# High and low parts of split weight blocks in one tile and one transfer

## The chip, the cores and the metric

The kernel runs on one NeuronCore of a Trainium2 chip. The metric is the device time of one execution in microseconds (us). Three runs of the kernel before gave 1211.52, 1212.36 and 1213.43 us; their median, 1212.36 us, is the time before. Engines are named as the profile names them: PE (TensorE) multiplies, PEld is its weight load, DVE (VectorE), ACT (ScalarE) and POOL (GpSimd) work elementwise, SP (SyncE) issues transfers. ACT and POOL issue transfers too; "SPq" and "ACTq" are those issues.

## The reference

One layer of a hybrid decoder step over 1024 prompt rows and 8 x 8 sample rows (1088 columns in all), model width 1024, float32:

```
h    = rmsnorm(x) * (1 + scale) + shift            # scale, shift, gate from silu(c) @ w_ada + b_ada
proj = h @ w_in                                    # 1024 -> 8224: u_pool, z_pool, z_ssm, xBC, dt, g
P    = (pool_mix(u_pool) * silu(z_pool)) @ w_pool_out          # 512 -> 1024
S    = gated_rmsnorm(SSD(conv(xBC)) + D*x, z_ssm) @ w_ssm_out  # 2048 -> 1024
x    = x + gate * ((sigmoid(g_pool) * P + sigmoid(g_ssm) * S) @ w_o)
out  = rmsnorm(x), and the new pooling, convolution and SSD states
```

SSD is a chunked state-space scan: 4 groups of heads, 8 chunks of 128 rows each.

## The kernel before, in words

**High and low parts.** Every float32 operand of a large product is split into a high part (a copy rounded to the fast float32r format, made by ACT) and a low part (operand minus high part, made by POOL or DVE). A product is then three products: high x high, low x high, high x low. A weight block is 128 x 512 numbers on 128 partitions, 2 KB a partition and 256 KB in all, for each part.

**Stages, in order of time.** (1) The first stage, up to about 90 us, has its order on all engines written out by hand. (2) Pairs of `w_in` columns go through a Strassen scheme (`strassen`, `product`, matmuls on line 411). Each block is split by `split` (line 142; ACT line 145, POOL line 148) into a `whi` and a `wlo` tile; the pool `wp` holds four of each, in turn. (3) Beside these pairs, `splits` (line 262) prepares `w_pool_out` and `w_ssm_out`: 40 blocks, each loaded (`begin`, line 275), scaled by the norm's gain and rounded (`halve`, lines 283 and 284), reduced to its low part on POOL (line 286), and stored to memory. `halve` stores the high part (line 285), `end` stores the low part (line 290), three steps later; a step is one product of 24 matmuls. All three issue on ACT's queue, and the raw tile `pw` has two buffers, the high tile `ph` has one. (4) From about 745 us the SSD chunks run, woven on PE with the products of the 40 prepared blocks (`gemm_`, matmuls on line 221). `ready` (line 304) loads each block's two parts back with two loads on SP's queue (lines 308 and 309), two units ahead of its use. (5) In the same stage `wo_splits` (line 1766) forms the Strassen sums of `w_o` on DVE (lines 1793 to 1804), 20 pieces of 128 x 512. `part` rounds a piece into a tile `ph` (three buffers, ACT line 1771), stores it on ACT's queue (line 1772), and POOL subtracts in place (line 1773). `out` stores the low part on SP's queue one step later (line 1778). (6) The tail multiplies by `w_o` and writes the outputs; there the buffers of `whi` and `wlo` are reused for the gate (`ga`), the sample rows (`sh`) and output rows (`w4`).

**What a chunk needs.** `chunk` (line 1492) loads `dec` (line 1225) three chunks ahead into one of three buffers; then ACT (lines 1504 and 1233), POOL (line 1229) and DVE (lines 1529 and 1531) turn it into the operands of `inner` (PE lines 1245 and 1248).

**Who sets the order.** In stages 1 and 4 to 5 the order on PE and SP is the order of the program text (`in_line`). Elsewhere, and on ACT, DVE and POOL in stages 4 to 6, a planner in the compiler orders instructions by a simulated timeline, with buffers of a tag handed out in turn when their last user is done. Each engine then runs its list strictly in order, its transfer issues included: an issue that waits for a buffer holds up what stands behind it on that engine.

Of the kernel before, what the change touches and what calls it, by code (L numbers as in the profile page):

```python
# [8 lines left out]
F32 = mybir.dt.float32  # L9
F32R = mybir.dt.float32r  # L10
AF = mybir.ActivationFunctionType
ALU = mybir.AluOpType
# [8 lines left out]
P = 128  # L21
# [25 lines left out]
def tile_pool_ssd_step(  # L47
# [5 lines left out]
    nc = tc.nc  # L53
    uid = [0]

    def nm(s):
        uid[0] += 1
        return f"{s}_{uid[0]}"

    cp = ctx.enter_context(tc.tile_pool(name="cp", bufs=1))  # L60
    wp = ctx.enter_context(tc.tile_pool(name="wp", bufs=3))
# [28 lines left out]
    def R(shape=(P, T), dt=F32):  # L90
        return hs.tile(list(shape), dt, tag="R", name=nm("R"), bufs=3)

    def Y4(pool, dt=F32R):
        return pool.tile([P, 4, T], dt, tag="Y", name=nm("Y"), bufs=2)
# [14 lines left out]
    load = nc.sync.dma_start  # L109
    store_ = nc.scalar.dma_start  # L110
    mm = nc.tensor.matmul
    act = nc.scalar.activation
# [26 lines left out]
    vT = const([P, 44], "vT")  # L139
    pscl = vT[:, 40:44]  # L140

    def split(raw, kept=None, ncols=P, eng=None):
        hi = wp.tile([P, 4, P], F32R, tag="whi", name=nm("whi"), bufs=4)
        lo = wp.tile([P, 4, P], F32R, tag="wlo", name=nm("wlo"), bufs=4)
        ins = act(hi[:, :, :ncols], raw[:, :, :ncols], AF.Copy)  # L145
        if kept is not None:
            kept.append(ins.ins)
        (eng or nc.gpsimd).tensor_tensor(lo[:, :, :ncols], raw[:, :, :ncols], hi[:, :, :ncols].bitcast(F32), ALU.subtract)  # L148
        return hi, lo
# [87 lines left out]
    def dram(name, shape, dt=F32):  # L237
        return dr.tile(list(shape), dt, tag=name, name=name)
# [23 lines left out]
    def splits():  # L262
        jobs = [(w_pool_out[m], None, wp_d[m]) for m in range(8)]
        jobs += [(w_ssm_out[g, m], 24 + 4 * g, ws_d[g][m])
                 for g in range(NG) for m in range(8)]
        raws, made = {}, [0]

        def paced():

            return highs[min(made[0] + 3, len(highs) - 1)]  # L270

        def begin(n):
            raws[n] = gas[0].tile([P, 4, P], F32, tag="pw", name=nm("pw"), bufs=2)
            with tc.issue_after(paced()):
                store_(raws[n], jobs[n][0])

        def halve(n):
            raw, gain = raws[n], jobs[n][1]
            hi = gas[0].tile([P, 4, P], F32R, tag="ph", name=nm("ph"), bufs=1)
            with tc.issue_after(paced()):  # L280
                if gain is not None:
                    for k in range(4):
                        act(raw[:, k], raw[:, k], AF.Copy, scale=vT[:, gain + k:gain + k + 1])
                act(hi, raw, AF.Copy)  # L284
                store_(jobs[n][2][:, 0], hi.bitcast(F32))
            nc.gpsimd.tensor_tensor(raw.bitcast(F32R), raw, hi.bitcast(F32), ALU.subtract)  # L286

        def end(n):
            with tc.issue_after(paced()):
                store_(jobs[n][2][:, 1], raws.pop(n))  # L290
        at = {}
        for n in range(len(jobs)):
            for f, step in ((end, 5), (begin, 0), (halve, 2)):
                at.setdefault(n * 17 // 5 + step, []).append((f, n))
        for t in range(max(at) + 1):
            made[0] += 1
            for f, n in sorted(at.get(t, ()), key=lambda x: x[1]):
                f(n)
            yield

    def wtiles():
        return [wp.tile([P, 4, P], F32R, tag=t, name=nm(t), bufs=4) for t in ("whi", "wlo")]

    def ready(d):
        def ws():
            with tc.high_priority(PRI):
                hi, lo = wtiles()
                load(hi.bitcast(F32), d[:, 0])
                load(lo.bitcast(F32), d[:, 1])
            return [(hi, lo)]  # L310
        return ws


# [197 lines left out]
    gas = []  # L511
# [113 lines left out]
    def first():  # L625
# [166 lines left out]
        raws, w, banks = {}, {}, {}  # L792
# [4 lines left out]
            load(raws[t, j], tiles_of(c)[:, 4 * j:4 * j + 4])  # L797

        def pieces(x, at):
            w[at] = [wp.tile([P, 4, P], F32R, tag=t, name=nm(t), bufs=4) for t in ("whi", "wlo")]  # L800
            return act(w[at][0], x, AF.Copy)

        def hi(t, j):
            pieces(raws[t, j], (t, j))
# [228 lines left out]
        def loads():  # L1033
            while waiting and said.issuperset(waiting[0][0]):
# [3 lines left out]
                     hi=hi, lo=lo, pr=pr, sgt=lambda: None, sg=sg, dwd=dwd, dU=dU, dL=dL, dR=dR, dUo=dUo,  # L1038
# [11 lines left out]
        for word in ORDER1:  # L1050
            fs = word.split(".")
            name, args = fs[0], [int(a) if a.isdigit() else a for a in fs[1:]]
            if name not in calls:
                i = len(name.rstrip("0123456789"))
                args.insert(0, int(name[i:]))
                name = name[:i]
# [396 lines left out]


    hst = [None] * NG

    CKL = ("sz", "v")

    def ckt(shape, tag, bufs=2):
        return (cl if tag in CKL else ca if tag in ("dec", "xb", "cE", "bc") else ck).tile(list(shape), F32, tag=tag, name=nm(tag), bufs=bufs)  # L1460
# [240 lines left out]
    cl = open_("cl", 2)  # L1701
    right = tc.tile_pool(name="ck", bufs=2, side="right", reuse_waits="tile")
    ck = right.__enter__()
    for shape, tag, bufs in (((P, 512), "ph", 3), ((P, P), "bt", 2), ((P, 8, 64), "xd", 2), ((P, 8, 64), "xw", 1),
                             ((P, 4, NS), "szs", 1), ((P, 512), "t2", 1), ((P, 512), "hst", 2)):
        ckt(shape, tag, bufs)

# [55 lines left out]
    wo_d = [dram(f"wo{k}", [P, 2, 4, 512]) for k in range(5)]  # L1763
    oB11, oT3, oT2, oT1, oT4 = range(5)

    def wo_splits():
        outs = []

        def part(o, k, t):
            hi = ck.tile([P, 512], F32R, tag="ph", name=nm("ph"), bufs=3)  # L1770
            act(hi, t, AF.Copy)
            store_(wo_d[o][:, 0, k], hi.bitcast(F32))
            nc.gpsimd.tensor_tensor(t.bitcast(F32R), t, hi.bitcast(F32), ALU.subtract)
            outs.append((wo_d[o][:, 1, k], t))

        def out():
            while outs:
                load(*outs.pop(0))
        left_, right_ = slice(0, 512), slice(512, 1024)

        def row(o):
            t = R()
            load(t[:, :D], w_o[0, o:o + P, :])
            return t
        up, dn = row(0), None
        yield
        for k in range(4):
            out()
            if k:
                part(oT3, k - 1, dn[:, right_])  # L1790
            old, dn = dn, row(512 + k * P)
            yield
            V.tensor_tensor(dn[:, right_], dn[:, right_], up[:, right_], ALU.subtract)
            V.tensor_tensor(up[:, right_], up[:, right_], up[:, left_], ALU.subtract)
            out()
            if k:
                part(oT4, k - 1, old[:, left_])
            yield
            t2 = ckt([P, 512], "t2", 1)
            V.tensor_tensor(t2, dn[:, right_], up[:, left_], ALU.add)  # L1800
            out()
            part(oT1, k, up[:, right_])
            yield
            V.tensor_tensor(dn[:, left_], t2, dn[:, left_], ALU.subtract)
            out()
            part(oB11, k, up[:, left_])
            yield
            out()
            part(oT2, k, t2)
            if k < 3:  # L1810
                up = row(k * P + P)
            yield
        out()
        part(oT3, 3, dn[:, right_])
        yield
        out()
        part(oT4, 3, dn[:, left_])
        yield
        out()
# [59 lines left out]
    def M(shape=(P, T), dt=F32):  # L1879
        return mp.tile(list(shape), dt, tag="m", name=nm("m"), bufs=2)  # L1880
# [10 lines left out]
    for o, n in GB:  # L1891
        s = slice(o, o + n)
# [18 lines left out]
    def b_load(o, y):  # L1911
        for t, c in ((0, lo_), (1, up_)):
            load(y[:, :, c].bitcast(F32), wo_d[o][:, t])
        return y
# [70 lines left out]
        return (pf, run)  # L1985
    run_units([tail_unit(m) for m in range(8)])

    def w2k(tag, dt=F32):
        return wp.tile([P, 512], dt, tag=tag, name=nm("half"), bufs=4)
    yt2 = b_load(oT2, Y4(hs))  # L1990

    lows = Y4(hs)
# [2 lines left out]
        nc.gpsimd.tensor_tensor(s2l[:, k], acc[k][:, lo_], s2h[:, k].bitcast(F32), ALU.subtract)  # L1995
    for k in range(4):
        nc.gpsimd.tensor_tensor(s1l[:, k], acc[k][:, up_], s1h[:, k].bitcast(F32), ALU.subtract)
    ga = [w2k("whi"), w2k("whi")]
    for half in range(2):
        load(ga[half], gate_d[0:1, half * 512:half * 512 + 512].squeeze(0).partition_broadcast(P))  # L2000

    sh = []
    for j in range(2):
        t = wp.tile([P, 4, P], F32R, tag="whi", name=nm("sh"), bufs=4)
        for k in range(4):
            a = acc[4 * j + k][:, SEQ:]
            act(t[:, k, 0:NS], a, AF.Copy)
            V.tensor_tensor(t[:, k, NS:P], a, t[:, k, 0:NS].bitcast(F32), ALU.subtract)
        sh.append(t)
# [6 lines left out]

    top = [R() for _ in range(3)] + [hs.tile([P, T], F32, tag="sq", name="top3", bufs=1)]
    C1 = [(t[:, lo_], t[:, up_]) for t in top]
    w4 = [w2k("wlo") for _ in range(4)]
    C2 = [(w4[0], w4[1]), (w4[2], w4[3])] + [(t[:, lo_], t[:, up_]) for t in (M(), M())]  # L2020
    bank = [0]

# [90 lines left out]
    for half in range(2):  # L2113
        c = slice(half * 512, half * 512 + 512)
# [168 lines left out]
```

## Time and profile before

| | |
|---|---|
| three runs, median | 1212.36 us |
| the profiled execution, device time | 1210.91 us |
| its span, first to last instruction | 1209.2 us |
| mean granted PE clock | 0.999 |
| instructions | 25239 |
| bytes read and written in memory | 173.31 MB, 87.73 MB |

The profile is of one execution. Its device time is 1.7 us more than its span. A row such as `L145 ACT ACTIVATE whi<-rawA` names a line of the kernel, the engine, the operation, and the tile written from the tile read. Busy time is the time in which an engine had an instruction of the program running; matmuls overlap each other, and their ends are modelled.

### The profile page before, as it was taken

What the parts mean: (1) busy time and instruction counts of PE and PEld (TensorE: products, weight loads), DVE (VectorE), ACT (ScalarE), POOL (GpSimd) and SP (SyncE); (2) the same over time, 40 slices, a digit from 0 to 9 for tenths busy, and PEclk for the clock granted to TensorE, in tenths of its full rate; (3) what the DMA queues carried; (4) which work ended last, traced back from release to release, by engine and by line L of the source; (5) the groups of instructions that cost most, each with busy time, mean ns of one, the idle gap of its engine ahead of it and who ended that gap; (6) DMA issues with size and microseconds to landing.
All of it is one profiled execution on the core that took longest, in us unless ns stands there. A gap on an engine that the chain in (4) does not pass through costs nothing.

```text
span 1209.2 us, 25239 instructions
## 1 busy us (share of the span) xinstructions
PE 1194.4 (99%) x9242; PEld 1118.5 (93%) x9242; DVE 924.8 (76%) x1535; ACT 649.1 (54%) x1479; POOL 763.4 (63%) x655
## 2 busy tenths in 40 slices
PE   9999999999999999999999999999999999999997
PEld 8879999999999999999989999988888888999885
DVE  6993788877989578877576555687878889679976
ACT  6864356565666557454434334566676657312435
POOL 1137878875988787764777776255767758423653
PEclk9999999999999999999999999999999999999999
DMA  9836445574556455454667767988879888585794
GB/s 352 306 132 219 136 144 184 164 228 146 171 174 198 160 164 172 135 169 131 208 227 238 245 223 247 320 309 262 270 250 294 277 284 285 173 326 166 235 212 154
DMA packets 167924, 262.72 MB, mean 217 GB/s; under 512 B 32880, under 2 KB 80760, under 8 KB 167800
## 3 DMA queue, kind: packets, MB, share of 16 engines
q1 hardware_dynamic: 90408, 166.01, 41.9%
q10 hardware_dynamic: 73232, 87.16, 21.2%
q0 software_dynamic: 4160, 7.94, 3.2%
q8 instruction: 73, 1.20, 0.4%
q14 instruction: 51, 0.42, 0.1%
HBM read 173.31 MB, written 87.73 MB: 216 GB/s over the span
## 4 chain that ended last, share of the span: by engine, by line
PE 87%; DVE 5%; DMA 3%; ACT 2%; issue 1%; POOL 0%; ACTq 0%; DVEq 0%; SPq 0%; POOLq 0%
PE mm L411 24%; PE ps L411 23%; PE mm L221 17%; PE pc L411 5%; PE ps L1245 3%; PE pc L1536 2%; PE ps L1248 2%; PE ps L2036 2%; PE ps L2034 2%; PE ps L2035 2%; PE ps L1511 1%; DMA dec<-acs_d 1%; DMA Y<-in_x_prompt 1%; PE ps L957 1%; DVE tf L643 1%
## 5 line engine op out<-in xcount | busy, mean ns | idle before, releaser
L148 POOL TENSOR_TENSOR wlo<-rawA,whi 128x512 fp32r<-128x512 f32 x120 | 174.7, 1461 | 80.7 <-ACT whi L145 79.4
L221 PE MATMUL mm<-Y,whi 128*128 128x352 f32 (+1 forms) x960 | 195.9, 334 | 0.8 <-DVE G L1969 0.6
L148 POOL TENSOR_TENSOR wlo<-raw,whi 128x512 fp32r<-128x512 f32 x90 | 149.8, 1673 | 64.6 <-ACT whi L145 62.2
L221 PEld LDWEIGHTS mm<-Y,whi 128*128 128x128 f32 x960 | 159.2, 188 | 7.6 <-issue 4.1
L1089 DVE SCALAR_TENSOR_TENSOR GA<-GA,cvT,GA 128x1112 f32<-128x1112 f32 x72 | 134.0, 1866 | 0.1
L411 PE MATMUL mm<-Y,whi 128*128 128x272 f32 x800 | 118.4, 290 | 0.0
L145 ACT ACTIVATE whi<-rawA 128x512 fp32r<-128x512 f32 x120 | 75.1, 627 | 79.6 <-PE ps L411 34.7
L411 PE MATMUL ps<-Y,whi 128*128 128x272 f32 x800 | 117.4, 289 | 0.0
L145 ACT ACTIVATE whi<-raw 128x512 fp32r<-128x512 f32 x90 | 56.0, 629 | 103.9 <-DVE raw L348 34.0
L411 PEld LDWEIGHTS mm<-Y,whi 128*128 128x128 f32 x800 | 106.9, 188 | 2.5 <-issue 1.0
L411 PEld LDWEIGHTS ps<-Y,whi 128*128 128x128 f32 x800 | 107.0, 188 | 0.8 <-issue 0.7
L221 PE MATMUL mm<-Y,wlo 128*128 128x352 f32 (+1 forms) x480 | 98.5, 327 | 0.0
L1233 ACT ACTIVATE dec<-dec,acT 128x128 f32<-128x128 f32 x256 | 78.8, 389 | 25.8 <-POOL dec L1229 25.8
L221 PEld LDWEIGHTS mm<-Y,wlo 128*128 128x128 f32 x480 | 81.7, 188 | 0.0
L286 POOL TENSOR_TENSOR pw<-pw,ph 128x512 fp32r<-128x512 f32 x40 | 67.0, 1675 | 13.4 <-ACT ph L284 12.5
L1468 POOL TENSOR_TENSOR Y<-xb,Y 128x512 fp32r<-128x512 f32 x32 | 41.2, 1287 | 53.7 <-ACT Y L1466 53.7
L411 PE MATMUL mm<-G,whi 128*128 128x272 f32 x480 | 71.2, 290 | 0.0
L411 PE MATMUL ps<-G,whi 128*128 128x272 f32 x480 | 70.3, 289 | 0.0
L411 PE MATMUL mm<-Y,wlo 128*128 128x272 f32 x400 | 66.8, 288 | 0.0
L411 PE MATMUL ps<-Y,wlo 128*128 128x272 f32 x400 | 66.6, 288 | 0.0
L411 PEld LDWEIGHTS mm<-G,whi 128*128 128x128 f32 x480 | 64.1, 188 | 1.2 <-issue 1.1
L411 PEld LDWEIGHTS ps<-G,whi 128*128 128x128 f32 x480 | 64.2, 188 | 0.3 <-issue 0.3
(579 smaller groups left out, 3130.5 us busy)
## 6 DMA issues: line engine op xcount, KB each, us to landing
rawA<-in_w_in SPq DMA_DIRECT2D x62, 512.0 KB
dec<-acs_d SPq DMA_DIRECT2D x32, 512.0 KB
xbc<-GA ACTq DMA_DIRECT2D x24, 512.0 KB
Y<-wo SPq DMA_DIRECT2D x10, 1024.0 KB
pw<-in_w_ssm_out ACTq DMA_DIRECT2D x32, 256.0 KB
ws<-ph ACTq DMA_DIRECT2D x32, 256.0 KB
ws<-pw ACTq DMA_DIRECT2D x32, 256.0 KB
h<-in_state_ssm SPq DMA_DIRECT2D x32, 256.0 KB
```

Source lines behind the costliest of these rows:

```text
L145: ins = act(hi[:, :, :ncols], raw[:, :, :ncols], AF.Copy)
L148: (eng or nc.gpsimd).tensor_tensor(lo[:, :, :ncols], raw[:, :, :ncols], hi[:, :, :ncols].bitcast(F32), ALU.subtract)
L221: mm(ps[:, :n], w[k // 4][h][:, k % 4, :], r[k][:, o:o + n], start=(j == 0), stop=(j == len(terms) - 1))
L286: nc.gpsimd.tensor_tensor(raw.bitcast(F32R), raw, hi.bitcast(F32), ALU.subtract)
L411: mm(p, w[j // 8][:, k], A(k, s)[j // 4 == 1], start=(j == 0), stop=(j == 11))
L1089: V.scalar_tensor_tensor(d[:, :n], rp[:, k:k + n], cvT[:, 24 * k + mc:24 * k + mc + 1], d[:, :n], ALU.mult, ALU.add)
L1233: act(dec[:, h], dec[:, h], AF.Exp, bias=acT[:, c, 8 * g + h:8 * g + h + 1], scale=-1.0)
L1245: mm(o[hh], xd[:S, 2 * q + hh, :], dec[:S, 2 * q + hh], start=True, stop=state is None)
L1248: mm(o[hh], state[:, h * 64:h * 64 + 64], cE[:, h], start=False, stop=True)
L1468: nc.gpsimd.tensor_tensor(yl[g][:, :, o:o + S], v, yhc.bitcast(F32), ALU.subtract)
L1536: mm(pu, bt, xw.rearrange("p h d -> p (h d)"), start=True, stop=True)
L2034: mm(ps, hi, y[:, k, c0:c0 + cw], start=(first and k == 0), stop=False)
```

## The change

A tile `w` of 4 KB a partition, with four buffers, holds both parts of a block: `[:, 0]` is the high part, `[:, 1]` the low one. It takes the place of `whi` and `wlo` everywhere (`split`, `pieces`, `ready`, and in the tail `ga`, `sh`, `w4`). In `splits` the raw block is loaded into the second half of a `pw` tile of 4 KB, ACT rounds into its first half, POOL subtracts in place in its second half, and `end` stores both with one transfer of 512 KB; the tile `ph` and the store in `halve` are gone. `ready` loads both parts with one transfer. In `wo_splits` a `ph` tile of 4 KB takes both parts (POOL writes the low part there instead of in place), and `out` stores both on SP's queue; ACT's store is gone.

```diff
+    def w_tile(dt=F32R):
+        return wp.tile([P, 2, 4, P], dt, tag="w", name=nm("w"), bufs=4)
+    def wtiles():
+        t = w_tile()
+        return t[:, 0], t[:, 1]
     def split(raw, kept=None, ncols=P, eng=None):
-        hi = wp.tile([P, 4, P], F32R, tag="whi", name=nm("whi"), bufs=4)
-        lo = wp.tile([P, 4, P], F32R, tag="wlo", name=nm("wlo"), bufs=4)
+        hi, lo = wtiles()
...
         def begin(n):
-            raws[n] = gas[0].tile([P, 4, P], F32, tag="pw", name=nm("pw"), bufs=2)
+            raws[n] = gas[0].tile([P, 2, 4, P], F32, tag="pw", name=nm("pw"), bufs=2)
             with tc.issue_after(paced()):
-                store_(raws[n], jobs[n][0])
+                store_(raws[n][:, 1], jobs[n][0])
         def halve(n):
-            raw, gain = raws[n], jobs[n][1]
-            hi = gas[0].tile([P, 4, P], F32R, tag="ph", name=nm("ph"), bufs=1)
+            (hi, raw), gain = (raws[n][:, t] for t in range(2)), jobs[n][1]
+            hi = hi.bitcast(F32R)
...
                 act(hi, raw, AF.Copy)
-                store_(jobs[n][2][:, 0], hi.bitcast(F32))
             nc.gpsimd.tensor_tensor(raw.bitcast(F32R), raw, hi.bitcast(F32), ALU.subtract)
         def end(n):
             with tc.issue_after(paced()):
-                store_(jobs[n][2][:, 1], raws.pop(n))
+                store_(jobs[n][2], raws.pop(n))
...
     def ready(d):
         def ws():
             with tc.high_priority(PRI):
-                hi, lo = wtiles()
-                load(hi.bitcast(F32), d[:, 0])
-                load(lo.bitcast(F32), d[:, 1])
-            return [(hi, lo)]
+                t = w_tile()
+                load(t.bitcast(F32), d)
+            return [(t[:, 0], t[:, 1])]
...
-    for shape, tag, bufs in (((P, 512), "ph", 3), ...
+    for shape, tag, bufs in (((P, 2, 512), "ph", PH), ...        # PH = 3
...
         def part(o, k, t):
-            hi = ck.tile([P, 512], F32R, tag="ph", name=nm("ph"), bufs=3)
-            act(hi, t, AF.Copy)
-            store_(wo_d[o][:, 0, k], hi.bitcast(F32))
-            nc.gpsimd.tensor_tensor(t.bitcast(F32R), t, hi.bitcast(F32), ALU.subtract)
-            outs.append((wo_d[o][:, 1, k], t))
+            both = ck.tile([P, 2, 512], F32R, tag="ph", name=nm("ph"), bufs=PH)
+            act(both[:, 0], t, AF.Copy)
+            nc.gpsimd.tensor_tensor(both[:, 1], t, both[:, 0].bitcast(F32), ALU.subtract)
+            outs.append((wo_d[o][:, :, k], both.bitcast(F32)))
...
-    ga = [w2k("whi"), w2k("whi")]
+    ga = w2k()                       # the two halves of one w tile
...
-    for j in range(2):
-        t = wp.tile([P, 4, P], F32R, tag="whi", name=nm("sh"), bufs=4)
+    for j, t in enumerate(wtiles()):
...
-    w4 = [w2k("wlo") for _ in range(4)]
+    w4 = w2k() + w2k()
```

More of the change, by code (lines that the diff above doesn't have):

```diff
@@ L299, in splits @@
             yield
-    def wtiles():
-        return [wp.tile([P, 4, P], F32R, tag=t, name=nm(t), bufs=4) for t in ("whi", "wlo")]
     def ready(d):
@@ L799, in pieces @@
         def pieces(x, at):
-            w[at] = [wp.tile([P, 4, P], F32R, tag=t, name=nm(t), bufs=4) for t in ("whi", "wlo")]
+            w[at] = wtiles()
             return act(w[at][0], x, AF.Copy)
@@ L1455, in tile_pool_ssd_step @@
     hst = [None] * NG
+    PH = 3
     CKL = ("sz", "v")
@@ L1703, in tile_pool_ssd_step @@
     ck = right.__enter__()
-    for shape, tag, bufs in (((P, 512), "ph", 3), ((P, P), "bt", 2), ((P, 8, 64), "xd", 2), ((P, 8, 64), "xw", 1),
+    for shape, tag, bufs in (((P, 2, 512), "ph", PH), ((P, P), "bt", 2), ((P, 8, 64), "xd", 2), ((P, 8, 64), "xw", 1),
                              ((P, 4, NS), "szs", 1), ((P, 512), "t2", 1), ((P, 512), "hst", 2)):
@@ L1986, in tile_pool_ssd_step, with w2k @@
     run_units([tail_unit(m) for m in range(8)])
-    def w2k(tag, dt=F32):
-        return wp.tile([P, 512], dt, tag=tag, name=nm("half"), bufs=4)
+    def w2k():
+        t = w_tile(F32).rearrange("p s k c -> p s (k c)")
+        return [t[:, 0], t[:, 1]]
     yt2 = b_load(oT2, Y4(hs))
```

## The prediction

> **What bounds the kernel now.** I read the profile's page first: busy time by engine, the transfer queues, the chain that ended last.
>
> ```profile
> span 1209.2 us, 25239 instructions
> PE 1194.4 (99%) x9242; PEld 1118.5 (93%) x9242; DVE 924.8 (76%) x1535; ACT 649.1 (54%) x1479; POOL 763.4 (63%) x655
> DMA packets 167924, 262.72 MB, mean 217 GB/s; under 512 B 32880, under 2 KB 80760, under 8 KB 167800
> q1 hardware_dynamic: 90408, 166.01, 41.9%
> q10 hardware_dynamic: 73232, 87.16, 21.2%
> PE 87%; DVE 5%; DMA 3%; ACT 2%; issue 1%; POOL 0%; ACTq 0%; DVEq 0%; SPq 0%; POOLq 0%
> L148 POOL TENSOR_TENSOR wlo<-rawA,whi 128x512 fp32r<-128x512 f32 x120 | 174.7, 1461 | 80.7 <-ACT whi L145 79.4
> L145 ACT ACTIVATE whi<-rawA 128x512 fp32r<-128x512 f32 x120 | 75.1, 627 | 79.6 <-PE ps L411 34.7
> ```
>
> PE is busy 99% of the span and is 87% of the chain. The edit touches no matmul. It touches transfers (SP's queue is q1, ACT's is q10) and the waits for buffers. So the first question is how much PE waits at all. The table of busy time by stretch answers it: the first row is everything between the hand-ordered stage and the last matmul, the others are the pair stage with its `splits`, the chunks with `wo_splits`, and the tail (columns: PE, PEld, DVE, ACT, POOL, PE clock, busy share of the transfer engines, GB/s).
>
> ```profile
> 90.00:1201.50 1111.50, 1109.30 (x8383) 1043.93 (x8381) 845.86 (x1366) 584.08 (x1354) 743.85 (x613) 1.00 0.66 213
> 84.00:488.00 404.00, 404.00 (x3189) 401.25 (x3188) 317.68 (x468) 233.06 (x535) 319.72 (x211) 1.00 0.55 174
> 865.00:1032.00 167.00, 166.53 (x1336) 147.74 (x1335) 141.27 (x242) 111.00 (x287) 123.12 (x140) 1.00 0.87 278
> 1091.00:1209.20 118.20, 109.96 (x526) 92.63 (x524) 100.13 (x159) 44.91 (x102) 55.16 (x45) 0.99 0.68 189
> ```
>
> From 90 to 1201.5 us PE is idle 1111.50 - 1109.30 = 2.2 us. In the pair stage it is never idle. The list of PE's waits after 90 us says whom it waited for (who, for what, us, times, longest):
>
> ```profile
> PE ps L1245 <- DVE dec L1306: 0.9, 1, 0.9
> PE mm L221 <- DVE G L1969: 0.6, 1, 0.6
> PE ps L1513 <- DVE cE L1531: 0.3, 1, 0.3
> PE mm L221 <- DVE Y L1567: 0.2, 1, 0.2
> ...
> 1201.23 0.27 PE L2036 MATMUL ps<-Y,s3l 128*128 128x256 f32 x1
> ```
>
> The last row, of PE's timeline, is its last matmul. Of the waits, not one is a wait for a weight part or its transfer. All that this edit can win by removing waits is bounded by those 2.2 us; the 7.7 us after the last matmul (1201.5 to 1209.2) are row sums and output stores, which it leaves alone. What it can lose has no such bound.
>
> **The change part by part.** The sum is made against the profiled execution: 1210.91 us, its span 1209.2 plus 1.7. The median of the runs, 1212.36, stands 1.45 us above it.
>
> *One ring of four tiles for both parts.* No instruction comes or goes. In every product the order of terms is high, low, high, so the high part is the last of the two to be read, and a shared tile comes free when the high tile did. What is made from it costs 0.63 us on ACT and 1.46 us on POOL a block (rows above). The cover: ACT stands idle until PE gives a buffer back, so blocks are made as early as the ring lets them:
>
> ```profile
> ACT whi L145 <- PE ps L411: 55.4, 42, 3.3
> ACT cE L1504 <- DMA dec<-acs_d: 14.1, 5, 5.3
> ```
>
> I cost it at 0. Without that cover a block would cost at most 0.63 + 1.46 = 2.1 us, where PE caught up with it. In the tail, `ga`, `sh` and `w4` need four shared tiles in place of four and four; the last of them waits for the same unit as before: 0. From below, nothing is there to win.
>
> *`splits`: 40 stores fewer on ACT's queue, twice the bytes in the 40 that remain, no `ph`.* The rows of the tiles `ph` and `ws` (minimum, median, maximum in ns):
>
> ```profile
> L285 ACTq DMA_DIRECT2D ws<-ph x32: 326/327/1777, 164.0 to 486.8; - x32
> L1772 ACTq DMA_DIRECT2D wo<-ph x20: 326/326/495, 866.9 to 1003.5; - x20
> L308 SPq DMA_DIRECT2D whi<-ws x32: 319/423/2186, 818.2 to 1090.9; - x32
> L309 SPq DMA_DIRECT2D wlo<-ws x32: 319/455/1636, 818.9 to 1090.4; - x32
> L1778 SPq DMA_DIRECT2D wo<-R x16: 320/609/747, 880.6 to 1030.9; - x16
> ```
>
> 40 x 0.327 = 13.1 us of issue leave ACT's queue. In the pair stage ACT is idle 404.0 - 233.1 = 171 us, so this is worth 0 to PE. The new cost: `begin` of block n+2 waits on ACT's queue until the store of block n has landed, and that store is now longer. Queue q10 took 21.2% of the span for 87.16 MB, that is 0.212 x 1209.2 = 256 us of all 16 engines, 0.77 us for 256 KB. ACT's timeline shows the tightest spacing, one store of 256 KB and the load that waited behind it:
>
> ```profile
> 205.61 0.33 ACTq L290 DMA_DIRECT2D ws<-pw  x1
> 207.65 0.34 ACTq L275 DMA_DIRECT2D pw<-in_w_ssm_out  x1
> ```
>
> So 2.04 us become some 2.8, with the ACT instructions behind it held 0.8 us longer. At most this happens 40 times, 31 us of ACT, under the 171 us it idles; a block is made three products ahead, and PE has no idle time in this stage at all. I take 0; the upper end, every 0.77 us reaching PE once at each of a few tight places, is 2 us.
>
> *`ready`: 40 loads in place of 80.* SP's queue is relieved of 40 x 0.455 = 18 us, and SPq is 0% of the chain: 0. The high part now lands with the low, about 0.77 us later. The last block is the one with the shortest work before it; SP issued it at 1090.87 and PE began on it at 1114.03:
>
> ```profile
> 1090.87 0.38 SPq L308 DMA_DIRECT2D whi<-ws  x1
> 1114.03 0.85 PE L221 MATMUL mm<-Y,whi 128*128 128x384 f32 x4
> ```
>
> 23 us of lead against 0.77: 0.
>
> *`wo_splits`: 20 stores leave ACT's queue, SP's 20 double.* ACT gains 20 x 0.326 = 6.5 us of issue; SP's issues take 0.6 us and perhaps twice that, 12 us in 165. POOL's subtraction is the same in size. Two things move. First, 20 x 256 KB go from ACT's queue to SP's, ahead of the chunks' own loads: 0.77 us each time. Second, a `ph` buffer is now free only when SP's store, one step after the rounding, has landed; before it was freed by ACT's own store and POOL. Today the five pieces of a step round are made in a burst; SP's stores follow much later and some 8 us apart:
>
> ```profile
> 866.29 1.13 ACT L1771 ACTIVATE ph<-R 128x512 fp32r<-128x512 f32 x2
> 870.07 1.14 ACT L1771 ACTIVATE ph<-R 128x512 fp32r<-128x512 f32 x2
> 880.63 0.61 SPq L1778 DMA_DIRECT2D wo<-R  x1
> 888.71 0.62 SPq L1778 DMA_DIRECT2D wo<-R  x1
> ```
>
> With three buffers the fourth and fifth piece of each burst must wait for a store: the burst spreads. What covers this is the margin with which a chunk's operands are ready. DVE's and PE's timelines at an ordinary chunk and at the tightest one (operand finished, first matmul that needs it):
>
> ```profile
> 871.38 1.21 DVE L1531 TENSOR_TENSOR cE<-cE,ps 128x1024 f32<-128x1024 f32 x1
> 875.29 0.44 PE L1245 MATMUL ps<-dec,xd 128*64 128x128 f32 x4
> 1013.85 1.21 DVE L1531 TENSOR_TENSOR cE<-cE,ps 128x1024 f32<-128x1024 f32 x1
> 1015.21 0.44 PE L1245 MATMUL ps<-dec,xd 128*64 128x128 f32 x4
> ```
>
> Margins of 875.29 - 872.59 = 2.70 and 1015.21 - 1015.06 = 0.15 us. And ACT was already held up to 5.3 us by a `dec` transfer (the second of ACT's wait rows above) in a stage where PE lost 0.5 us in 167. I take -0.2 us, a smoother ACT and POOL giving back a little of that 0.5. The ends are -2.2 (every wait gone) and +6, from the first rival.
>
> *Pools.* `pw` needs 2 KB a partition more, the pool `ck` 6 KB more, so other tiles shift onto other predecessors. No row shows an address; the bound is the same margin, 0 to 2.7 us hidden, and I take 0.
>
> Sum: 0 + 0 + 0 - 0.2 + 0 = -0.2 us, 1210.7 for a profiled execution and **1212.2 us** for the median. Not measurable: two medians of this kernel tell about 0.2%, 2.4 us, apart.
>
> **The rivals.** *Slower: ACT held by the `ph` ring.* Place: 865 to 1032 us. A rounding that the planner puts on ACT before the store three pieces back has landed holds ACT, and with it the chunk's exponentials. The chain that ended last shows what a landing takes here:
>
> ```profile
> 894.47 5.56 DMA dec<-acs_d
> 914.10 6.58 DMA sz<-z
> 922.45 5.15 DMA dec<-acs_d
> ```
>
> 6.58 + 0.77 = 7.4 us for 512 KB. One such hold costs PE 7.4 - 2.7 = 4.7 us: 1217 us; two make 1221. It decides as soon as one hold exceeds 2.7 + 2.4 = 5.1 us. For it: 17 of 20 pieces now wait for a landing, and the planner's clock is not the chip's. Against: the 5.3 us hold that cost nothing, and stores 8 us apart, so that three pieces back is usually long landed.
>
> *Slower: SP's ring.* Every transfer engine serves SP's and ACT's queue side by side; moving 20 high parts puts them in line ahead of `dec` and `sz`. The Trainium skill, "DMA: Bandwidth & Descriptors", section "Queues, rings and completion order", says that each engine takes the queue rows in turn, a packet at a time, which would let the chunks' loads overtake a store on ACT's row but not one on their own; no run here shows the turns. From the rows: 0.77 us behind each store, which costs PE 0.77 - 0.15 = 0.6 us at a chunk as tight as the last one above and nothing at an ordinary one. Four tight chunks in a row make 2.4 us, 1215; one or two leave no measurable change.
>
> *Faster: the bursts were the trouble.* If spreading the pieces and freeing 60 ACT issues removes all of PE's 2.2 us and evens the tail a little, 1209.8. Against: two of the four waits (0.6 and 0.2 us) have nothing to do with it.
>
> *It doesn't do what it says:* a transfer of both parts is cut into the same 2 KB packets. Then the packet count stands, and the time too.
>
> **How the numbers follow.** No measurable change 0.69 (the forecast, with the fourth rival in it). Slower 0.23: the `ph` ring 0.14, SP's ring 0.05, 0.04 for shifted pools and a reordered plan. Faster 0.08, since its cap of 2.2 us lies below what can be told. The likeliest case alone spans 1209.9 to 1214.8; the range runs from all waits gone (1212.36 - 2.2 and a run's spread, 1209.2) to one full hold with some of the rest, 1218.0, and leaves out two holds.
>
> **What would show it.** Packets fall by 80 x 128 = 10240, and by a few a transfer for 100 transfers fewer; q1 rises by 20 x 256 KB = 5.24 MB to 171.3, q10 falls to 81.9. PE from 90 to 1201.5 us stays idle for about 2 us. The `ph` copies come singly. The forecast is wrong if PE waits for `ph`, `dec` or `cE` in the chunks, if a wait for `w` appears anywhere, or if PE's order changes.

## The result and the profile after

The kernel after takes 1208.93 us (median of 7 runs, 1208.48 to 1211.12); the kernel before, on the same chip, 1213.73 us (7 runs, 1211.52 to 1215.66). The ratio is 0.9964, 95% interval 0.9952 to 0.9975. A second set, of 9 and 31 runs, gave 0.9969 (0.9959 to 0.9980). The forecast was 1212.2 us, no measurable change; the kernel became 0.3 to 0.4% faster.

The page of the profile after (device time 1208.48 us) first:

```profile
span 1206.8 us, 24905 instructions
PE 1194.0 (99%) x9242; PEld 1119.8 (93%) x9242; DVE 911.0 (75%) x1535; ACT 645.7 (54%) x1479; POOL 775.0 (64%) x655
DMA packets 156081, 262.68 MB, mean 218 GB/s; under 512 B 31280, under 2 KB 79160, under 8 KB 155960
q1 hardware_dynamic: 87208, 171.25, 42.9%
q10 hardware_dynamic: 64592, 81.91, 19.7%
PE 91%; DVE 4%; DMA 2%; ACT 2%; issue 1%; SPq 0%; ACTq 0%; DVEq 0%
```

PE does the same work (1194.0 us busy, before 1194.4) in a shorter span, and its share of the chain rose from 87% to 91%. So it waits less. Where, the table by stretch shows (columns as before); first the kernel before in 488 to 745 us, the second half of the stage of pairs, which the prediction had not cut out; then the kernel after, the same stretch, the chunks with `wo_splits`, and everything from 90 us to its last matmul:

```profile
488.00:745.00 257.00, 256.07 (x2060) 242.43 (x2059) 169.24 (x318) 113.58 (x236) 171.88 (x136) 1.00 0.59 196
```

```profile
488.00:745.00 257.00, 257.00 (x2068) 243.42 (x2067) 167.47 (x318) 112.06 (x236) 174.55 (x136) 1.00 0.60 198
865.00:1032.00 167.00, 167.00 (x1359) 148.11 (x1360) 141.17 (x242) 111.41 (x291) 124.05 (x140) 1.00 0.83 276
90.00:1199.30 1109.30, 1108.49 (x8381) 1043.67 (x8379) 832.16 (x1366) 580.61 (x1354) 755.59 (x613) 1.00 0.66 214
```

PE's idle time between 90 us and the last matmul fell from 2.2 to 0.8 us; none of what is left lies in the two stages of these rows. The list of PE's waits after 86 us has two rows over 0.2 us left:

```profile
PE mm L227 <- DVE G L1970: 0.6, 1, 0.6
PE mm L227 <- DVE Y L1569: 0.3, 1, 0.3
```

Gone are the samples' wait for `dec` (0.9 us, near 620 us) and the chunk's wait for `cE` (0.3 us); both remaining rows stood in the profile before. Between these two profiles PE's idle time fell by 2.2 - 0.8 = 1.4 us, of the 1210.91 - 1208.48 = 2.4 us between the executions. But the profiled execution of before (1210.91 us) was faster than any of its seven runs in the comparison, so its 0.9 us need not be the usual size of that wait.

### The profile page after: what moved, and what is told of

Its sections match the earlier page's. It is cut to its first block, busy times and chain, and to the rows that moved or that the text cites. A ratio compares the mean times of both kernels' runs of the same rounds, so it can differ in the third digit from the quotient of the medians.

```text
span 1206.8 us, 24905 instructions
## 1 busy us (share of the span) xinstructions
PE 1194.0 (99%) x9242; PEld 1119.8 (93%) x9242; DVE 911.0 (75%) x1535; ACT 645.7 (54%) x1479; POOL 775.0 (64%) x655
## 3 DMA queue, kind: packets, MB, share of 16 engines
q1 hardware_dynamic: 87208, 171.25, 42.9%
q10 hardware_dynamic: 64592, 81.91, 19.7%
## 4 chain that ended last, share of the span: by engine, by line
PE 91%; DVE 4%; DMA 2%; ACT 2%; issue 1%; SPq 0%; ACTq 0%; DVEq 0%
PE mm L412 24%; PE ps L412 23%; PE mm L227 19%; PE pc L412 5%; PE ps L1246 3%; PE pc L1538 2%; PE ps L1249 2%; PE ps L2037 2%; PE ps L2035 2%; PE ps L2036 2%; PE ps L1513 1%; DMA Y<-in_x_prompt 1%; PE ps L958 1%; DVE tf L644 1%; PE pc L1335 1%
## 5 line engine op out<-in xcount | busy, mean ns | idle before, releaser
L227 PE MATMUL mm<-Y,w 128*128 128x352 f32 (+1 forms) x1440 | 255.4, 331 | 0.8 <-DVE G L1970 0.6
L227 PEld LDWEIGHTS mm<-Y,w 128*128 128x128 f32 x1440 | 235.3, 188 | 7.6 <-issue 4.6
L154 POOL TENSOR_TENSOR w<-rawA,w 128x512 fp32r<-128x512 f32 x120 | 181.7, 1518 | 78.5 <-ACT w L151 73.8
L154 POOL TENSOR_TENSOR w<-raw,w 128x512 fp32r<-128x512 f32 x90 | 157.9, 1761 | 62.6 <-ACT w L151 62.4
L412 PE MATMUL mm<-Y,w 128*128 128x272 f32 x1200 | 168.7, 289 | 0.0
L412 PE MATMUL ps<-Y,w 128*128 128x272 f32 x1200 | 167.8, 289 | 0.0
L412 PEld LDWEIGHTS mm<-Y,w 128*128 128x128 f32 x1200 | 156.8, 188 | 2.6 <-issue 1.0
L412 PEld LDWEIGHTS ps<-Y,w 128*128 128x128 f32 x1200 | 157.1, 188 | 0.8 <-issue 0.6
L151 ACT ACTIVATE w<-rawA 128x512 fp32r<-128x512 f32 x120 | 75.2, 627 | 95.4 <-PE ps L412 56.1
L151 ACT ACTIVATE w<-raw 128x512 fp32r<-128x512 f32 x90 | 56.0, 628 | 104.3 <-DVE raw L349 36.4
L412 PE MATMUL mm<-G,w 128*128 128x272 f32 x720 | 101.2, 289 | 0.0
L412 PE MATMUL ps<-G,w 128*128 128x272 f32 x720 | 100.6, 289 | 0.0
L412 PEld LDWEIGHTS ps<-G,w 128*128 128x128 f32 x720 | 94.4, 188 | 0.3 <-issue 0.3
```

Of the source, the lines that this page charges most:

```text
L227: mm(ps[:, :n], w[k // 4][h][:, k % 4, :], r[k][:, o:o + n], start=(j == 0), stop=(j == len(terms) - 1))
L412: mm(p, w[j // 8][:, k], A(k, s)[j // 4 == 1], start=(j == 0), stop=(j == 11))
```

## The experiments

All changes are named against the kernel before (`e_`) or the kernel after (`a_`). Ratios are to the kernel before in the same set of runs.

**The same kernel, profiled again.** No edit.

> The kernel before, unchanged, in one more profiled execution. Theory A (PE waits that depend on when transfers land, so they differ from run to run): PE idle between 90 us and its last matmul is not 2.2 us again but between 2 and 7 us, and the waits stand at other places or with other lengths; its time is 1212 to 1215 us. Theory B (a fixed plan gives fixed waits): the same four waits, 2.0 us in all, and 1210.9 us within 0.3.

1212.54 us, the same order of instructions on every engine. PE's waits:

```profile
PE ps L1245 <- DVE dec L1306: 2.6, 1, 2.6
PE ps L1513 <- DVE cE L1531: 0.6, 1, 0.6
```

The samples' wait was 0.9 us and is 2.6. It is not a fixed cost of the kernel. The chain that ended last, cut out around that place in this run (start, us, what), names what varies:

```profile
615.57 6.36 DMA gp<-u
622.03 0.44 DVE u L420
622.46 0.60 DVE dec L1306
623.20 0.68 PE ps L1245 x16
```

ACT stores a strip `u` (the tag `u2` of the Strassen sums, one buffer). DVE's next sum into that buffer (L420) waits until the store has landed, and `dec` for the samples stands behind it on DVE. The same step of the chain in the first profile of before:

```profile
615.71 4.71 DMA gp<-u
```

There 4.71 us of landing go with a wait of 0.9; here 6.36 with 2.6; in three kernels below 5.18 with 1.4, 5.62 with 1.8 and 5.66 with 1.9. In all five the wait is the landing less 3.8 us.

**The parts of the change, one by one.** Only `w_o`'s pieces:

```diff
-            hi = ck.tile([P, 512], F32R, tag="ph", name=nm("ph"), bufs=3)
+            both = ck.tile([P, 2, 512], F32R, tag="ph", name=nm("ph"), bufs=3)
...
-            store_(wo_d[o][:, 0, k], hi.bitcast(F32))
...
+            outs.append((wo_d[o][:, :, k], both.bitcast(F32)))
```

> Only the pieces of w_o share a tile and a store on SP's queue; all else as before. If the gain comes from the chunk stage (pieces no longer in bursts, ACT rid of 20 issues): 0.9975 to 0.9985 of before, PE without the wait near 932 us, the wait near 620 us still there. If the gain is the new plan of the pair stage: 0.999 to 1.000. The slower rival of the prediction (ACT held by the ph ring): above 1.002.

1212.3 us, ratio 0.9987 (0.9976 to 0.9998). The samples' wait is still there (1.8 us).

Everything but `w_o`'s pieces (the diff of the change without its hunks in `part` and the pool of `ph`):

> All of the change except the pieces of w_o. If the chunk stage gives the gain: 0.999 to 1.000 of before, the waits near 932 and 1014 us still there. If the pair stage's plan and the weight transfers give it: 0.9965 to 0.998, the wait near 620 us gone.

1209.82 us, 0.9967 (0.9955 to 0.9978). So most of the gain is not in the `w_o` part.

Only the shared tile, with two loads and two stores a block as before:

```diff
     def split(raw, kept=None, ncols=P, eng=None):
-        hi = wp.tile([P, 4, P], F32R, tag="whi", name=nm("whi"), bufs=4)
-        lo = wp.tile([P, 4, P], F32R, tag="wlo", name=nm("wlo"), bufs=4)
+        hi, lo = wtiles()
...
     def ready(d):     # unchanged: two loads, into the halves of one w tile
```

> Only the shared tile: high and low part in one buffer, but two loads and two stores a block as before, w_o as before. No byte moves otherwise, so a theory of transfers says 1.000 (0.9995 to 1.0005). A theory of the plan (ACT, DVE and POOL in another order because the ring is another) says that the wait near 620 us goes, 0.999, and that other waits may come.

1210.43 us, 0.9978 (0.9967 to 0.9989). The samples' wait is gone; in the chunks PE waits 1.3 us once for `cE`:

```profile
PE ps L1517 <- DVE cE L1535: 1.3, 1, 1.3
PE ps L1248 <- DVE cE L1535: 0.5, 1, 0.5
```

The shared tile and one load a block:

```diff
-                load(hi.bitcast(F32), d[:, 0])
-                load(lo.bitcast(F32), d[:, 1])
+                t = w_tile()
+                load(t.bitcast(F32), d)
```

> The shared tile with one load a block in place of two, stores of splits and w_o as before. If SP's 40 issues are hidden, as the prediction has it: as the shared tile alone, 0.9978 (0.997 to 0.9985). If one load in place of two is worth something in the chunk stage: below 0.997.

1210.4 us, 0.9979 (0.9969 to 0.9989): as the shared tile alone. The 40 loads saved are worth nothing that these runs can tell.

Only the merged stores of `splits`:

```diff
-                store_(jobs[n][2][:, 0], hi.bitcast(F32))
...
-                store_(jobs[n][2][:, 1], raws.pop(n))
+                store_(jobs[n][2], raws.pop(n))
```

> The kernel before with the stores of splits alone merged (40 stores of 512 KB on ACT's queue, no ph tile there), two tiles and two loads as before. PE never waits in that stage, so a theory of waits says 1.000 (0.999 to 1.001) unless the plan of the pairs moves the wait near 620 us. A theory in which fewer transfers help by themselves says 0.998 to 0.999.

1212.63 us, 0.9999 (0.9990 to 1.0008). The 40 stores saved alone are worth nothing that can be told either, and the samples' wait (1.4 us) stays. One comparison leaves room: all but `w_o`'s part, with loads and stores merged, has 1209.82 us where the shared tile alone has 1210.43 us in the same set of runs. Their intervals overlap.

**The wait taken away without a shared tile.** Two buffers for the tag `u2` in the kernel before, so that DVE's next sum needs no landing:

```diff
-            return pa.tile([P, 2, SB], F32, tag=tag, name=nm(tag))
+            return pa.tile([P, 2, SB], F32, tag=tag, name=nm(tag), bufs=2 if tag == "u2" else 1)
```

(and the same number of buffers where the tag is opened in two other places; PE, DVE, POOL and SP keep their order)

> The kernel before with one edit that is not in the change: the Strassen sum u2 has two buffers, so DVE need not wait until the store of the pair before has landed. If that wait near 620 us (0.9, 2.6 and 1.8 us in three profiles of kernels with the old ring) is what the shared tile took away, this gives what the shared tile alone gave: 0.9975 to 0.9985, and no PE wait near 620 us. If the shared tile helps by something else: 0.9995 to 1.0005.

1210.12 us, 0.9979 (0.9969 to 0.9989), the ratio of the shared tile. PE's waits:

```profile
PE mm L221 <- DVE G L1969: 0.5, 1, 0.5
PE mm L221 <- DVE Y L1567: 0.3, 1, 0.3
```

So that wait is worth about 0.2%, 0.0021 x 1213 = 2.5 us in the timed runs. The five profiles that have it show 0.9 to 2.6 us of waiting, 1.7 on average. The rest can come from the clock. In two of the five, those of `e_wo` and `e_order`, PE's granted clock falls to 0.50 for 3.41 us, beginning 1.6 and 0.4 us after PE went on; in none of the fourteen profiles does it fall anywhere else between 8 and 1201 us. The stretch in `e_wo` (columns as before):

```profile
624.00:628.00 4.00, 4.00 (x22) 4.00 (x21) 0.97 (x3) 0.86 (x2) 0.00 (x1) 0.57 0.63 156
```

There twelve matmuls of a product take 2.21 and 2.52 us where the first profile of before has 1.69 and 1.50. At half the clock, 3.41 us lose 1.7 us. Two such drops in five add 0.7 us to the mean wait of 1.7, together 2.4 us: an estimate from five profiles, close to the measured 2.5. The timed runs point the same way: in the set of the kernel after's second profile, the mean granted clock is 0.9975 over the 31 runs of the kernel before and 0.9986 over the 9 of the kernel after.

**Five buffers for `w_o`'s pieces in the kernel after.** `PH = 3` becomes `PH = 5`.

> The changed kernel with five ph buffers in place of three, so that the five pieces of w_o of a round can be made in a burst again. If the gain of the w_o part is that the ring spaces the pieces: the bursts at 866, 907, 952 and 996 us are back, PE waits near 932 or 1014 us again, 0.9970 to 0.9980 of before, that is 0.001 above the changed kernel. If the gain is ACT's 20 issues less: as the changed kernel, 0.9964.

1209.72 us, 0.9971 (0.9961 to 0.9981). The pieces come mostly in bursts again (at 865 to 868, 907 to 908, 954 to 956 and 994 to 995 us, with a single one or two after each but the first), and PE waits once in the chunks:

```profile
PE ps L1515 <- DMA sz<-z: 0.5, 1, 0.5
```

The direction fits a gain from spreading them, the size (0.9971 against 0.9964 and 0.9969) is inside the intervals.

**Why does the shared tile take the wait away?** First theory: by the order of ACT's work. In the kernel before, ACT does a high copy and then the two halves of `u` ahead of the store; in the kernel after, half of `u`, the copy, the other half. The kernel before with that order, and no engine but ACT reordered:

```diff
-            act(buf[:, s], buf[:, s], func)
+            with tc.high_priority(PRIO): act(buf[:, s], buf[:, s], func)
```

> The kernel before, with one thing changed: silu and sigmoid of the stored strips get the high priority in the planner, so that near the samples ACT does u, whi, u and then the store of u, as the kernel after does (u, w, u), where the kernel before does whi, u, u. PE's, DVE's, POOL's and SP's instructions keep their order; both parts of a weight block keep their two tiles and two transfers. Theory A, that the shared tile won its time by ACT's new order in front of the store of u: the wait of the samples' first matmul at L1245 for DVE's decay (0.9 to 2.6 us with the old order) is gone or under 0.5 us, the store is issued about 1.3 us earlier, and the ratio is 0.998 to 0.999. Theory B, that it is the shared tile itself or the fewer transfers: the ratio is 1.000 and the wait is still there.

The ratio, 0.9989 (0.9977 to 1.0001), decides nothing, but the trace does. ACT's timeline of this kernel (start, us, what, in brackets the idle time before it and who ended it), and PE's wait:

```profile
614.33 0.43 ACT L500 ACTIVATE u<-u 128x272 f32<-128x272 f32 x1 [3.99 <-DVE u L425]
614.67 0.62 ACT L145 ACTIVATE whi<-rawA 128x512 fp32r<-128x512 f32 x1
615.19 0.41 ACT L500 ACTIVATE u<-u 128x272 f32<-128x272 f32 x1
615.64 0.35 ACTq L502 DMA_DIRECT2D gp<-u  x1
```

```profile
PE ps L1245 <- DVE dec L1306: 1.9, 1, 1.9
```

The order is that of the kernel after, and still the store is issued at 615.64 us, where the kernel before has 615.71. ACT stood idle for 4 us, waiting for DVE. The theory falls: DVE is late, not ACT. So the question moves back to DVE. Its timeline, with those of PE, ACT and POOL, in the kernel before:

```profile
607.00 1.16 PE L411 MATMUL ps<-G,whi 128*128 128x272 f32 x8
608.00 0.67 PE L411 MATMUL ps<-G,wlo 128*128 128x272 f32 x4
...
608.25 0.63 ACT L145 ACTIVATE whi<-raw 128x512 fp32r<-128x512 f32 x1 [0.16 <-PE ps L411]
...
607.80 2.52 POOL L148 TENSOR_TENSOR wlo<-raw,whi 128x512 fp32r<-128x512 f32 x2 [3.58 <-ACT whi L145]
...
609.05 1.82 DVE L348 TENSOR_TENSOR rawA<-rawA,rawA 128x512 f32<-128x512 f32 x1
611.49 0.58 DVE L1313 COPY cz<-hst 128x32 f32<-128x32 f32 x1
614.12 0.42 DVE L425 TENSOR_TENSOR u<-u,ps 128x272 f32<-128x272 f32 x1
```

and in the kernel after:

```profile
606.78 1.67 PE L412 MATMUL ps<-G,w 128*128 128x272 f32 x12
...
608.54 0.63 ACT L151 ACTIVATE w<-raw 128x512 fp32r<-128x512 f32 x1 [0.66 <-PE ps L412]
...
607.59 1.28 POOL L154 TENSOR_TENSOR w<-raw,w 128x512 fp32r<-128x512 f32 x1 [2.59 <-ACT w L151]
609.25 1.42 POOL L154 TENSOR_TENSOR w<-raw,w 128x512 fp32r<-128x512 f32 x1 [0.38 <-ACT w L151]
...
608.84 0.68 DVE L349 TENSOR_TENSOR rawA<-rawA,rawA 128x512 f32<-128x512 f32 x1
610.57 0.18 DVE L1314 COPY cz<-hst 128x32 f32<-128x32 f32 x1
613.11 0.44 DVE L426 TENSOR_TENSOR u<-u,ps 128x272 f32<-128x272 f32 x1 [0.23 <-PE ps L412]
...
614.36 0.35 ACTq L503 DMA_DIRECT2D gp<-u  x1
```

Read PE's rows first. A product reads its weight's high part eight times and then the low part four times: the low part is last. The separate high tile came free after the eighth matmul (607.00 + 1.16 = 608.16), and ACT filled it at 608.25. The shared tile comes free after the twelfth (606.78 + 1.67 = 608.45), and ACT fills it at 608.54. With the copy early, POOL makes two low parts back to back, 607.80 to 610.32. With the copy late, POOL pauses between them, from 608.87 to 609.25. DVE's weight sum is issued just there. In the kernel before it finishes only at 610.87, half a microsecond after POOL's second low part: 1.82 us. In the kernel after it slips into POOL's pause: 0.68 us, and POOL's second part takes 1.42 in place of 1.28. The 1.14 us saved on the sum, and 0.4 on the copy `cz`, bring `u` forward and with it the store: issued at 614.36 in place of 615.71 (0.2 us of this is that all of PE's work stands earlier there). The Trainium skill, "SBUF — State Buffer", section "SBUF: two separate sides", says that DVE and POOL share a pair of ports, held exclusively for a whole instruction by whichever starts first, which a DVE operation with two inputs in SBUF needs too while POOL reads there; the 1.82 against 0.68 us agree.

The earlier store is not the whole of it. DVE's next sum into `u`, and the samples' first matmul, before and then after:

```profile
620.51 0.44 DVE L420 TENSOR_TENSOR u<-s,mm 128x272 f32<-128x272 f32 x1 [1.39 <-DMA gp<-u]
621.68 0.68 PE L1245 MATMUL ps<-dec,xd 64*64 64x64 f32 x16 [0.93 <-DVE dec L1306]
```

```profile
618.80 0.42 DVE L421 TENSOR_TENSOR u<-s,mm 128x272 f32<-128x272 f32 x1
620.47 0.68 PE L1246 MATMUL ps<-dec,xd 64*64 64x64 f32 x16
```

In the kernel before the matmul starts 621.68 - 615.71 - 4.71 = 1.26 us after the landing. In the kernel after it starts at 620.47, so PE stays free of this wait as long as the landing takes less than 620.47 - 614.36 - 1.26 = 4.85 us. With the landings of the seven profiles that have separate tiles, 4.71 to 6.36 us, up to 1.5 us of the wait would be left. But in the seven with the shared tile the store lands in 3.74 to 4.14 us.

The trace's records of transfers show what differs. A store's landing is signalled in sixteen parts. With separate tiles fifteen are in after 3.67 to 4.42 us, and one comes late, alone. A packet of 16 KB runs beside this store, on a queue that the page lists as `instruction`, 73 packets and 1.20 MB in the whole kernel, before and after:

```profile
q8 instruction: 73, 1.20, 0.4%
```

With separate tiles this packet starts 0.86 to 3.84 us after the store's issue and lasts 0.88 to 1.91 us; in five of the seven the store's delayed packets go on within 0.02 us of its end. With the shared tile it starts 3.90 to 4.25 us after the issue, and the store's last packet has ended by then (after 3.34 to 3.74 us). So the late part of the landing goes with this packet, and the size of PE's wait with it. The records do not name the transfer engine of a packet, and no run shows why the packet comes when it does. That the store now passes ahead of it is nothing the edit aimed at. How much of the gain comes from the earlier store and how much from the shorter landing was not separated.

That sum takes 1.82 or 1.83 us in all seven profiled kernels that have separate tiles (the two of before, and the ones with only `w_o`'s part, only the stores, ACT's order, `u2`, and `u2` with `w_o`'s part) and 0.68 or 0.69 in all seven with the shared tile. What was not run is a kernel with separate tiles whose high part is read last, which would separate the late release from everything else in the shared tile. So the link from the shared tile over the later copy to the earlier store is read from the traces and not shown by an experiment of its own.

**Do the causes add up?** Two buffers for `u2` and `w_o`'s part, with the weight blocks as before (both diffs stand above):

> The kernel before, with two buffers for the Strassen sum u2 and with w_o's high and low parts in one tile and one transfer; the weight blocks keep their two tiles and transfers. If the whole gain of the change is these two causes, the wait near 620 us and the waits in the chunk stage, the ratio is that of the change, 0.996 to 0.997, and the profile has no wait at L1245 and single copies of w_o's pieces. If merged blocks bring something of their own, it stays at 0.998.

1209.72 us, 0.9973 (0.9963 to 0.9982); its list of PE's waits has nothing over 0.5 us. The kernel after with two buffers for `u2`:

> The kernel after, with two buffers for the Strassen sum u2. If the change has already removed the wait that the single buffer causes near 620 us, nothing is left to win: the ratio is that of the kernel after, 0.996 to 0.997. If the two gains are separate causes, they add up to 0.994 to 0.995.

1209.54 us, 0.9971 (0.9959 to 0.9982). And the kernel after again, beside these:

> The kernel after once more, on the chip and beside the runs of the three others, as their direct comparison: 0.996 to 0.997. Its PE shows no wait over 0.5 us between 90 and 1201 us if its order leaves slack for the landings; a wait of about 1 us in the chunk stage if the profile after was merely a lucky one.

1209.32 us, 0.9969 (0.9959 to 0.9980), with the same two waits of PE as in the first profile after. The second buffer adds nothing that can be told to the kernel after, as it should if it takes away the same wait. The two edits together give 0.9973 without a shared weight tile, within 0.0004 of the whole change in the same set. No version beat the kernel after.

What stays unsettled is the share of `w_o`'s part. Alone it gives 0.9987, on top of `u2` it moves 0.9979 to 0.9973, and the change without it has 0.9967. These differences are 0.03 to 0.13%, each inside the intervals, so it may be nothing. The traces show what it does. ACT's timeline in the kernel before, and below it in the kernel after:

```profile
907.02 1.15 ACT L1771 ACTIVATE ph<-R 128x512 fp32r<-128x512 f32 x2 [1.64 <-DVE R L1794]
908.08 0.61 ACT L1771 ACTIVATE ph<-t 128x512 fp32r<-128x512 f32 x1
912.90 0.61 ACT L1771 ACTIVATE ph<-R 128x512 fp32r<-128x512 f32 x1
913.79 0.62 ACT L1771 ACTIVATE ph<-R 128x512 fp32r<-128x512 f32 x1
```

```profile
906.06 0.63 ACT L1773 ACTIVATE ph<-R 128x512 fp32r<-128x512 f32 x1 [1.69 <-DVE R L1795]
914.16 0.62 ACT L1773 ACTIVATE ph<-R 128x512 fp32r<-128x512 f32 x1
919.16 0.63 ACT L1773 ACTIVATE ph<-t 128x512 fp32r<-128x512 f32 x1 [1.96 <-DMA wo<-ph]
```

In the kernel before five pieces fall within 7 us. With three buffers the fourth needs the landing of the first one's store, and in the second profile of before ACT stands idle for it:

```profile
913.82 0.63 ACT L1771 ACTIVATE ph<-R 128x512 fp32r<-128x512 f32 x1 [0.69 <-DMA wo<-ph]
```

In the kernel after, all but the first three of the twenty come one by one. The nine profiles with bursts have 0 to 1.8 us of PE's waits in the chunks (0 once), the five with single pieces 0, 0, 0, 0 and 1.1.

## Why the prediction was right or wrong

**What held.** No matmul waits for a weight part. Packets fell by 11843: the 10240 forecast, and 1600 under 512 B for 100 transfers fewer. q1 and q10 moved 171.25 and 81.91 MB, as forecast. `splits` and `ready`, costed at 0, measured 0.9999 and no difference between 0.9979 and 0.9978. The rival that a transfer of both parts saves no packets is out. Two of the signs that the prediction named against itself did appear, in small: PE's order differs at two places (near 153 us and from 1110 to 1119 us, where neighbouring products changed places), and one weight load waits 0.8 us for ACT's `w` copy, near 590 us, while PE is not idle. The time did not: 1208.93 us lies 0.3 us below the lower end of the range, 1209.2.

**The slower rivals.** "ACT held by the `ph` ring": its place was right and its price was not. ACT waits for a piece's store three times in the whole kernel after, 3.7 us in all, the longest 1.96 us above, under the 2.7 us of margin that the prediction read. It had overlooked that ACT was already held there before, because the bursts already ran out of the three buffers: 1.2 us once in the first profile of before, 3.0 us in two waits in the second. "SP's ring" cost nothing that PE shows: in neither profile of the kernel after has it a wait over 0.2 us in the chunks.

**The step that failed: "One ring of four tiles for both parts".** It said that "in every product the order of terms is high, low, high, so the high part is the last of the two to be read, and a shared tile comes free when the high tile did", and "From below, nothing is there to win." The order is high, high, low: `product` takes `w[j // 8]` for the twelve matmuls, and PE's timeline shows eight reads of `whi` and then four of `wlo`. So the shared tile comes free 4 matmuls later. On its own that looks like a small loss for ACT, whose waits for products (L145 and L151 behind `ps`) rose from 55.4 to 89.7 us; with those behind `mm` and `pc` they rose from 102.7 to 128.5 us:

```profile
ACT w L151 <- PE ps L412: 89.7, 61, 3.3
```

PE still never waits for a block. But a copy that comes later leaves POOL a pause in which DVE gets its sum done, and that sum stood ahead of the store whose landing held PE. The store, now earlier, also landed sooner, which has no term in the prediction. The term measured -0.22% (0.9978), about -2.7 us, where the prediction put 0. That it is a gain and not a loss looks like luck of this place in the plan: the late copy opened POOL's pause just where DVE's sum was due.

**The second step that failed: the cap.** "All that this edit can win by removing waits is bounded by those 2.2 us." That number came from one execution of 1210.91 us, below all seven later runs of the same kernel. The samples' wait, 0.9 us in it, was 2.6 in the next profile and 1.4 to 1.9 in three kernels that leave it alone. With the mean of the five, 1.7 us, the bound is 3.0 us, and it leaves out the time that a drop of the clock behind the wait costs (1.7 us in two of the five). So the chance of "faster" was much too small. The rival "Faster: the bursts were the trouble" had the direction, but the cause that it names measured only 0.03 to 0.13%; most of the gain came from a wait that the prediction had listed and taken for untouched.

**The term `wo_splits`**, -0.2 us with ends at -2.2 and +6: measured -0.03 to -0.13%, -0.4 to -1.6 us, inside its ends and inside the noise.

## What to carry to other kernels

When two buffers become one, look up in the trace which of them was read last: the shared buffer has the later of the two release times, and what refills it can shift by that. A cap on what can be won needs more than one profile when a wait ends with a transfer's landing; look at who stands behind that landing on its engine, and try a second buffer for it first (one more buffer for `u2` gave 0.2% here; no gain from the 80 transfers saved could be told). Such a wait can cost more than its length: look at the granted clock behind it. And where two kernels issue the same work in nearly the same order, compare the durations of the same instruction on DVE and POOL: one that takes 1.8 us in place of 0.7 points to a collision.

## What the runs showed of the hardware

- A DVE sum of two 128x512 float32 tiles took 0.68 us when POOL paused and 1.82 us when POOL did two subtractions of the same size back to back beside it.
- The landing of one and the same store of 272 KB took 4.71 to 6.36 us in the seven profiles in which a 16 KB packet of the instruction queue ran 0.86 to 3.84 us after its issue, and 3.74 to 4.14 us in the seven in which that packet came after the store's last. In the five with a wait of PE behind the landing, the wait was the landing less 3.8 us.
- Behind a wait of PE of 1.8 and 1.9 us the granted clock fell to 0.50 for 3.41 us in two profiles; behind waits of 0.9, 1.4 and 2.6 us at the same place it did not in three others.
- 80 transfers and 10240 packets fewer in the weight blocks (the merged stores and the merged loads) changed the time by nothing that can be told, each by itself: 0.9999 for the stores, 0.9979 against 0.9978 for the loads.
